# New tokens of the token-major products: 64 high beside 64 low parts in two float32r passes

## The chip, the cores and the metric

One core of a Trainium2 chip runs one program. The time is that of one execution on the device in microseconds (us). Of the core's engines, TensorE (PE) multiplies matrices, VectorE (DVE), ScalarE (ACT) and GpSimd (POOL) work on tiles, and SyncE (SP) issues most DMA transfers. Each engine takes its instructions in its own fixed order and waits at semaphores for the others.

## The reference

One step of a hybrid decoder with two layers, on 512 prompt tokens (one sequence) and 64 new tokens (8 samples of 8), which share all weights; D = 1024, everything in float32. Layer 0 projects its input to the queries, keys and values of sparse attention A (an indexer chooses keys by top-k) and of forgetting attention B, which read paged caches; layer 1 is a gMLP. A ConvFFN follows each. What the change touches is the projection `h @ w` of all 576 tokens, where the result is wanted with tokens in the rows:

```
def project_ab(h, w_in, b_f, pos):
    ...
    qa, ka, va, qi, ki, wi, qb, kb, vb, fb = jnp.split(h @ w_in, offs, axis=-1)
...
def chunk_gate_inputs(h, w_in, lnv_g, lnv_b):
    z = jax.nn.gelu(h @ w_in, approximate=False)
    u, v = jnp.split(z, 2, axis=-1)
    return u, layer_norm(v, lnv_g, lnv_b)
```

Here `h = x*(1+scale)+shift` with a scale and shift for each sequence. The indexer's queries (`qi`), `vb`, `va`, `ka`, `qa` and the gMLP's `v` are the products with tokens in the rows ("token-major"): 1024 columns of w in `w_ab`, 1536 in `w_aa`, 2048 in `w_v`.

## The kernel before

Activations lie feature-major: 1024 features in 8 blocks (kb) of 128 partitions, 576 tokens beside each other, the 512 of the prompt first, then the 64 new ones. A float32 product is made of float32r values: an operand is split into a high part (`xh`, `wh`), rounded by ScalarE, and the low rest (`xl`, `wl`), subtracted by VectorE or GpSimd (`split_to` for activations, `weights` for a unit of 128x1024 weights; L251 casts, L254 subtracts). `mm3` (L283 to L285) then makes three passes: high by high, high by low, low by high. Each of the tiles `wr` (raw weights), `wh` and `wl` has three buffers; a buffer is loaded again when its last reader has finished.

In a token-major product (`token_product`, `token_unit`) the tokens are the stationary operand, 128 at a time, and the weights are streamed; a unit of weights serves 1024/n blocks k of n columns, n = 512 for `w_ab` (two products of 4 units: indexer queries, then values of B), n = 256 for `w_aa` (`project_a`, 6 products of 2 units) and `w_v` (`gmlp`, 8 products of 2 units). Token blocks 0 to 3 go through `mm3`. The last block, tb = 4, has only the 64 new tokens; its product is one plain float32 matmul for each k, of a raw copy `xn` (64 columns) with the raw weights `wr` (L682). Even k add up in PSUM rows 0 to 63, odd k in rows 64 to 127 (`tile_position` chooses the half of the array), and `both_halves` adds the two.

`xn` is written by GpSimd for layer 0 (`modulate`, L430: eight copies of 128x64, one for each kb) and, for the gMLP, by `Norm.finish`, where it is the value before the split. `Norm.finish` runs at each norm that has a successor: into the first FFN, into the gMLP, and into the second FFN. Both norms' splits are L741 (new tokens) and L161/L162 (prompt). The gMLP's first units run at its entrance, mixed with the norm's transposes (L83, L153); from about 1151 us its units follow each other alone.

Behind the `w_ab` product of the indexer's queries hangs a chain: rotary turn (L705 to L708, VectorE), transposes (L721), copies of the new tokens' query rows (L942, GpSimd), their transposes (L945, PE), gathers of indexer keys (L1106, GpSimd's queue), scores (L1109 to L1122), and a top-k on VectorE (from L1048), beside which B's projections and the projections of A run. Pages of the caches are loaded by SyncE meanwhile.

The order on each engine is not written by hand: a scheduler lays it out when the kernel is built, from the program text, priorities and its own simulation of the engines. A change in a few instructions therefore moves others as well.

Of the kernel before, what the change touches and what calls it, by code (L numbers as in the profile page):

```python
# [10 lines left out]
F32 = mybir.dt.float32  # L11
# [48 lines left out]
class Norm:  # L60
# [56 lines left out]
    def finish(self, part):  # L117
# [19 lines left out]
        if part:  # L137
# [8 lines left out]
            nc.vector.tensor_tensor(t, t, wide(self.offs), op=OP.add)  # L146
            net.split_to(*(w[:, :, NP:] for w in self.out), self.xn)
        for k0 in range(0, KB, 2):
            ks = slice(k0, k0 + 2)
# [53 lines left out]
class Net:  # L203
# [217 lines left out]
    def modulate(self, xk, sc1, sh, kb, pool):  # L421
# [7 lines left out]
        nc.vector.tensor_tensor(ts, ts, sh[:, kb, 1:9, None].to_broadcast([P, 8, 8]), op=OP.add)  # L429
        nc.gpsimd.tensor_copy(self.xn[:, kb], t[:, NP:])  # L430
        self.split_to(*(x[:, kb] for x in self.xhl), t)


# [114 lines left out]
    def gmlp(self, x, last, psum, pool, xp, *norm):  # L548

        nc, a, xs, xn = self.nc, self.a, last.xs, last.xn  # L550
        g1 = self.plus_one(1, 2, xp, "g1")
# [19 lines left out]
        def lead():  # L571
            c, u = todo.pop(0)
            if u == 0:
                led[c] = [], [psum.tile([P, 2, 256], F32, name=name, bufs=b) for name, b in (("acc", 4), ("tc", 2))]
            units, accs = led[c]
            units.append(self.weights(a["w_v"][c, u], 1024))
            self.token_unit({tb: accs[tb // 4][:, tb % 2] for tb in (2, 3, 4)}, units[u], u, 256, xs, xn, True, (2, 3, 4))

# [3 lines left out]
        for c in range(8):  # L582
            first = None
            for u in range(2):
# [3 lines left out]
                first = first or psum.tile([P, 2, 256], F32, name="acc", bufs=4)  # L588
                self.token_unit([first[:, 0], first[:, 1]], units[u], u, 256, xs, xn, True, (0, 1))
            accs = [first] + led.pop(c)[1]  # L590
# [73 lines left out]

    def token_unit(self, accs, w, u, n, xs, xn, shared=False, tbs=range(5), between=None):

# [4 lines left out]
        for tb in tbs:  # L671
            for j in range(per):
# [7 lines left out]
                else:  # L680
                    c = 64 * (k % 2)
                    self.nc.tensor.matmul(accs[tb][c:c + NS], xn[:, k], wk[2], start=k < 2, stop=k >= KB - 2,  # L682
                                          tile_position=(0, c))
            if between:
                between()

    def token_product(self, accs, srcs, xs, xn, n, between=None, shared=False, before=None):

        for u, src in enumerate(srcs):
            w = self.weights(src, 1024)  # L690
            if before:
                before(u)
            self.token_unit(accs, w, u, n, xs, xn, shared, between=between)

# [55 lines left out]
    def project(self, keep, pool, room, psum, free):  # L750
# [5 lines left out]
        xs = self.xs = [self.halves(tuple(x[:, kb] for x in self.xhl)) for kb in range(KB)]  # L756
        self.xn = pool.tile([P, KB, NS], F32, name="xn")
        self.sc1 = pool.tile([P, KB, 9], F32, name="sc1")
# [56 lines left out]
        toks = self.five(psum)  # L815
        self.token_product(toks, [a["w_ab"][0, u] for u in range(4)], xs, self.xn, 512, None, False, before)
        qit = self.pair(tmp, [P, 4, NP], "qit")
# [5 lines left out]
        kd = tmp.tile([P, 5, P], F32, name="kd")  # L823
        rt = tmp.tile([P, 5, 64], F32, name="rt8")
        for n, t0, t1 in ((P, 0, 4), (NS, 4, 5)):
# [18 lines left out]
        for ci, name in enumerate(("qi", "vb")):  # L844
            accs = toks
            if ci:
                accs = self.five(psum)
                self.token_product(accs, [a["w_ab"][ci, u] for u in range(4)], xs, self.xn, 512, between)
            for tb in range(5):
# [50 lines left out]
    def project_a(self, pool, psum, xs, between):  # L900
# [3 lines left out]
        for c, name in enumerate(("va", "ka", "qa")):  # L904
            for half in range(2):
                cols = slice(256 * half, 256 * half + 256)
                accs = [psum.tile([P, 2, 256], F32, name="s", bufs=5) for _ in range(3)]
                self.token_product([accs[tb // 2][:, tb % 2] for tb in range(5)], [a["w_aa"][c, half, u] for u in range(2)],
                                   xs, self.xn, 256, between, True)
                for i in range(3):  # L910
# [702 lines left out]
```

## Time and profile before

| | us |
|---|---|
| three timed runs | 1953.62, 1954.88, 1960.26 (median 1954.88) |
| profiled execution, its own time | 1954.99 |
| its span (first to last instruction) | 1952.9 |
| PE busy | 1830.8 (94% of the span), 14456 matmul records |
| DVE, ACT, POOL busy | 1185.3, 736.5, 374.0 |
| mean granted clock of PE | 0.968 of full speed |

The profile shows one execution. A row of the timeline has the start, the duration, the engine, the line, the operation with output and inputs, the shape, and a count where equal instructions follow each other (x8); brackets hold the time that the engine stood idle before the row and what ended it. The end of a matmul is modelled, so the distance from start to start is the better measure. In the trace one float32 matmul stands as two records of L682 each; a float32r matmul as one.

### The profile page before, as it was taken

To read this page: it belongs to the slowest core of one execution; us is meant where nothing else is said; L and a number is where in the kernel's file an instruction comes from. 1 tells how busy PE (TensorE), PEld (TensorE's weight loads), DVE (VectorE), ACT (ScalarE), POOL (GpSimd) and SP (SyncE) were. 2 spreads that over 40 slices of the span, in tenths; PEclk is the share of its full clock that TensorE was granted. 3 is DMA by queue.
4 is the path that set the end of the run, shared out by engine and by line. 5 is a ranking of instruction groups with operands and counts; after the bars stand their busy time and mean duration, and the time that the engine had idled before them with its cause. 6 is when DMAs were issued, how large, how long until landed. Compare 5 with 4: busy or idle time off the path is not lost. (4 is left out here: it accounts for less than half of the span.)

```text
span 1952.9 us, 37037 instructions
## 1 busy us (share of the span) xinstructions
PE 1830.8 (94%) x14456; PEld 1627.1 (83%) x14456; DVE 1185.3 (61%) x2437; ACT 736.5 (38%) x1372; POOL 374.0 (19%) x521
## 2 busy tenths in 40 slices
PE   6889999898889899999999999899998999999996
PEld 4646877555559899999999899799997999999995
DVE  3549963455449754545456953875468555565577
ACT  2323222255444533424344433122224535344543
POOL 2323511110025300100012330430013201010124
PEclk9989999999899999999999999899998999999998
DMA  8446587797864345353543333321222231313242
GB/s 287 128 151 219 179 263 244 238 304 240 279 232 141 118 132 181 126 181 128 193 140 109 107 101 98 94 70 59 82 97 86 71 103 62 102 50 114 87 139 92
DMA packets 140032, 284.39 MB, mean 146 GB/s; under 512 B 32338, under 2 KB 42002, under 8 KB 139794
## 3 DMA queue, kind: packets, MB, share of 16 engines
q1 hardware_dynamic: 139138, 279.67, 43.8%
q0 software_dynamic: 720, 2.36, 0.4%
q8 instruction: 114, 1.87, 0.4%
q14 instruction: 60, 0.49, 0.1%
HBM read 271.04 MB, written 10.94 MB: 144 GB/s over the span
## 5 line engine op out<-in xcount | busy, mean ns | idle before, releaser
L298 PE MATMUL acc<-xh,wh 128*128 128x256 f32 (+1 forms) x1664 | 499.9, 301 | 3.0 <-ACT xh L161 1.7
L298 PE MATMUL acc<-xl,wh 128*128 128x256 f32 (+1 forms) x1664 | 497.5, 299 | 4.8 <-DVE xl L162 4.8
L298 PE MATMUL acc<-xh,wl 128*128 128x256 f32 (+1 forms) x1664 | 496.0, 298 | 6.0 <-DVE wl L254 6.0
L251 ACT CAST wh<-wr 128x1024 fp32r<-128x1024 f32 (+2 forms) x276 | 260.7, 949 | 536.6 <-PE acc L298 371.6
L254 DVE TENSOR_TENSOR wl<-wr,wh 128x1024 fp32r<-128x1024 f32 (+2 forms) x211 | 229.4, 1090 | 240.2 <-ACT wh L251 214.4
L298 PEld LDWEIGHTS acc<-xh,wh 128*128 128x128 f32 x1664 | 319.9, 192 | 11.5 <-issue 6.2
L298 PEld LDWEIGHTS acc<-xh,wl 128*128 128x128 f32 x1664 | 319.9, 192 | 6.6 <-DVE wl L254 6.2
L298 PEld LDWEIGHTS acc<-xl,wh 128*128 128x128 f32 x1664 | 319.9, 192 | 6.2 <-DVE xl L162 6.0
L254 POOL TENSOR_TENSOR wl<-wr,wh 128x1024 fp32r<-128x1024 f32 x65 | 160.5, 2469 | 531.2 <-ACT wh L251 513.4
L298 PE MATMUL acc<-gh,wl 128*128 128x256 f32 (+1 forms) x704 | 207.7, 298 | 1.6 <-DVE wl L254 1.6
L298 PE MATMUL acc<-gl,wh 128*128 128x256 f32 (+1 forms) x704 | 208.8, 298 | 0.0
L298 PE MATMUL acc<-gh,wh 128*128 128x256 f32 (+1 forms) x704 | 207.5, 300 | 0.4 <-ACT gh L740 0.4
L439 DVE SCALAR_TENSOR_TENSOR x<-acc,g,x 128x256 f32<-128x256 f32 x256 | 119.7, 476 | 118.3 <-PE acc L298 112.9
L525 DVE SCALAR_TENSOR_TENSOR y<-up,wc,y 128x592 f32<-128x592 f32 x176 | 150.6, 856 | 34.0 <-ACT y L522 29.9
L298 PEld LDWEIGHTS acc<-gh,wh 128*128 128x128 f32 x704 | 132.4, 189 | 5.5 <-issue 2.9
L298 PEld LDWEIGHTS acc<-gh,wl 128*128 128x128 f32 x704 | 132.6, 189 | 2.9 <-DVE wl L254 1.9
L298 PEld LDWEIGHTS acc<-gl,wh 128*128 128x128 f32 x704 | 133.3, 189 | 0.3 <-DVE gl L741 0.2
L518 POOL COPY tail<-up 128x2 f32<-128x2 f32 x88 | 26.1, 297 | 519.4 <-ACT up L516 519.1
L516 ACT COPY up<-acc 128x256 f32<-128x256 f32 x176 | 65.1, 371 | 130.0 <-PE acc L298 121.8
L283 PE MATMUL s<-wh,xh 128*128 128x256 f32 (+1 forms) x256 | 82.4, 330 | 3.2 <-ACT wh L251 3.2
L522 ACT ACTIVATE y<-up,wc 128x592 f32<-128x592 f32 x88 | 77.8, 884 | 9.2 <-POOL up L514 1.1
L285 PE MATMUL s<-wh,xl 128*128 128x256 f32 (+1 forms) x256 | 81.0, 317 | 0.0
(435 smaller groups left out, 3513.5 us busy)
## 6 DMA issues: line engine op xcount, KB each, us to landing
wr<-in_w_up SPq DMA_DIRECT2D x88, 512.0 KB
wr<-in_w_down SPq DMA_DIRECT2D x32, 512.0 KB
wh<-in_w_mod SPq DMA_DIRECT2D x30, 512.0 KB
wl<-in_w_mod SPq DMA_DIRECT2D x30, 512.0 KB
wr<-in_w_mod SPq DMA_DIRECT2D x28, 512.0 KB
own<-in_kT_b SPq DMA_DIRECT2D x48, 256.0 KB
own<-in_v_b SPq DMA_DIRECT2D x44, 256.0 KB
wr<-in_w_down SPq DMA_DIRECT2D x32, 320.0 KB
```

The costliest lines, as they stand in the source:

```text
L251: nc.scalar.copy(h, r)
L254: (nc.vector if low == "v" else nc.gpsimd).tensor_sub(l, r, h.bitcast(F32))
L283: mm(out, sh, mh, start=start, stop=False)
L285: mm(out, sl, mh, start=False, stop=stop)
L298: mm(acc, w[:, k * P:(k + 1) * P], m, start=i == 0, stop=i == n - 1)
L439: nc.vector.scalar_tensor_tensor(xp, acc[:, :256], g1[:, ob, 0:1], xp, op0=OP.mult, op1=OP.add)
L516: nc.scalar.copy(u[:, 2 + 256 * part:258 + 256 * part], accs[part][:, :256])
L518: nc.gpsimd.tensor_copy(tail[:, blk, 0:2], u[:, NP:NP + 2])
L522: nc.scalar.activation(y[:, :n], u[:, 0:n], AF.Identity, bias=wc[:, 3, blk:blk + 1], scale=wc[:, 0, blk:blk + 1])
L525: nc.vector.scalar_tensor_tensor(y[:, :n], u[:, k:k + n], wc[:, k, blk:blk + 1], y[:, :n], op0=OP.mult, op1=OP.add)
```

## The change

`xn`, where a product reads it, becomes `xst`: for each block k 64 columns of the high parts of the new tokens and beside them 64 columns of the low parts, float32r, copied by GpSimd after the split. The product of the last token block becomes two passes for each k, `xst` (128 columns) by `wh` and by `wl`: rows 0 to 63 of PSUM get the high tokens' products, rows 64 to 127 the low tokens', and `both_halves` adds them as before. `low` by `low` is now included. The raw weights are no longer read by PE. In the norm, `xn` stays as the value before the split and `xst` is new beside it. A scratch tile `rt8` of the projection is replaced by the shared one `rt`.

```diff
@@ -145,6 +145,9 @@
             nc.scalar.copy(x[:, :, NP:], ps)
             nc.vector.tensor_tensor(t, t, wide(self.offs), op=OP.add)
             net.split_to(*(w[:, :, NP:] for w in self.out), self.xn)
+            self.xst = xp.tile([P, KB, 2, NS], F32R, name="xst")
+            for i, w in enumerate(self.out):
+                nc.gpsimd.tensor_copy(self.xst[:, :, i], w[:, :, NP:])
         for k0 in range(0, KB, 2):
             ks = slice(k0, k0 + 2)
             pt = psum.tile([P, 2, 2, P], F32, name="tp", bufs=2)
@@ -427,8 +430,9 @@
         nc.vector.tensor_tensor(ts, xk[:, NP:].rearrange("p (b q) -> p b q", b=8),
                                 sc1[:, kb, 1:9, None].to_broadcast([P, 8, 8]), op=OP.mult)
         nc.vector.tensor_tensor(ts, ts, sh[:, kb, 1:9, None].to_broadcast([P, 8, 8]), op=OP.add)
-        nc.gpsimd.tensor_copy(self.xn[:, kb], t[:, NP:])
         self.split_to(*(x[:, kb] for x in self.xhl), t)
+        for i, x in enumerate(self.xhl):
+            nc.gpsimd.tensor_copy(self.xst[:, kb, i], x[:, kb, NP:])
 
 
     def add_gated(self, x, acc, g1, ob, pool, part):
@@ -547,7 +551,7 @@
 
     def gmlp(self, x, last, psum, pool, xp, *norm):
 
-        nc, a, xs, xn = self.nc, self.a, last.xs, last.xn
+        nc, a, xs, xst = self.nc, self.a, last.xs, last.xst
         g1 = self.plus_one(1, 2, xp, "g1")
 
         ws = pool.tile([P, 8, P], F32, name="ws")
@@ -574,7 +578,7 @@
                 led[c] = [], [psum.tile([P, 2, 256], F32, name=name, bufs=b) for name, b in (("acc", 4), ("tc", 2))]
             units, accs = led[c]
             units.append(self.weights(a["w_v"][c, u], 1024))
-            self.token_unit({tb: accs[tb // 4][:, tb % 2] for tb in (2, 3, 4)}, units[u], u, 256, xs, xn, True, (2, 3, 4))
+            self.token_unit({tb: accs[tb // 4][:, tb % 2] for tb in (2, 3, 4)}, units[u], u, 256, xs, xst, True, (2, 3, 4))
 
 
         for _ in range(3):
@@ -586,7 +590,7 @@
                     lead()
                 units, accs = led[c]
                 first = first or psum.tile([P, 2, 256], F32, name="acc", bufs=4)
-                self.token_unit([first[:, 0], first[:, 1]], units[u], u, 256, xs, xn, True, (0, 1))
+                self.token_unit([first[:, 0], first[:, 1]], units[u], u, 256, xs, xst, True, (0, 1))
             accs = [first] + led.pop(c)[1]
             for i in range(3):
                 n, nb = (P, 2) if i < 2 else (NS, 1)
@@ -662,7 +666,7 @@
 
         return bass.AP(tensor=ap.tensor, offset=ap.offset, ap=[[0, n]] + [list(s) for s in ap.ap[1:]])
 
-    def token_unit(self, accs, w, u, n, xs, xn, shared=False, tbs=range(5), between=None):
+    def token_unit(self, accs, w, u, n, xs, xst, shared=False, tbs=range(5), between=None):
 
 
 
@@ -678,19 +682,19 @@
                     self.mm3(accs[tb], *x, *wk[:2], k == 0 and not (shared and tb % 2),
                              k == KB - 1 and not (shared and tb % 2 == 0))
                 else:
-                    c = 64 * (k % 2)
-                    self.nc.tensor.matmul(accs[tb][c:c + NS], xn[:, k], wk[2], start=k < 2, stop=k >= KB - 2,
-                                          tile_position=(0, c))
+                    x = xst[:, k].rearrange("p i n -> p (i n)")
+                    for i in range(2):
+                        self.nc.tensor.matmul(accs[tb], x, wk[i], start=k + i == 0, stop=k + i == KB)
             if between:
                 between()
 
-    def token_product(self, accs, srcs, xs, xn, n, between=None, shared=False, before=None):
+    def token_product(self, accs, srcs, xs, xst, n, between=None, shared=False, before=None):
 
         for u, src in enumerate(srcs):
             w = self.weights(src, 1024)
             if before:
                 before(u)
-            self.token_unit(accs, w, u, n, xs, xn, shared, between=between)
+            self.token_unit(accs, w, u, n, xs, xst, shared, between=between)
 
     def both_halves(self, acc, out):
 
@@ -754,7 +758,7 @@
         tmp = room.enter_context(tmp)
         self.xhl = self.pair(pool, [P, KB, T], "x")
         xs = self.xs = [self.halves(tuple(x[:, kb] for x in self.xhl)) for kb in range(KB)]
-        self.xn = pool.tile([P, KB, NS], F32, name="xn")
+        self.xst = pool.tile([P, KB, 2, NS], F32R, name="xst")
         self.sc1 = pool.tile([P, KB, 9], F32, name="sc1")
         for q in range(2):
             self.begin(q, pool, tmp, psum)
@@ -813,7 +817,7 @@
                              *xs[k][part], k == 0, k == KB - 1)
 
         toks = self.five(psum)
-        self.token_product(toks, [a["w_ab"][0, u] for u in range(4)], xs, self.xn, 512, None, False, before)
+        self.token_product(toks, [a["w_ab"][0, u] for u in range(4)], xs, self.xst, 512, None, False, before)
         qit = self.pair(tmp, [P, 4, NP], "qit")
 
         smt = pool.tile([P, T], F32, name="tmp", bufs=3)[:80]
@@ -821,7 +825,7 @@
             nc.scalar.copy(smt[:, t0:t1], acc[:80, :t1 - t0])
         raw = tmp.tile([P, 5, 80], F32, name="ev8")
         kd = tmp.tile([P, 5, P], F32, name="kd")
-        rt = tmp.tile([P, 5, 64], F32, name="rt8")
+        rt = pool.tile([P, 512], F32, name="rt", bufs=2)[:, :320].rearrange("p (t d) -> p t d", t=5)
         for n, t0, t1 in ((P, 0, 4), (NS, 4, 5)):
             t = psum.tile([P, 4, 80], F32, name="tp", bufs=2)
             for tb in range(t0, t1):
@@ -845,7 +849,7 @@
             accs = toks
             if ci:
                 accs = self.five(psum)
-                self.token_product(accs, [a["w_ab"][ci, u] for u in range(4)], xs, self.xn, 512, between)
+                self.token_product(accs, [a["w_ab"][ci, u] for u in range(4)], xs, self.xst, 512, between)
             for tb in range(5):
                 n = self.tok(tb)[1]
                 rows = slice(tb * P, tb * P + n)
@@ -906,7 +910,7 @@
                 cols = slice(256 * half, 256 * half + 256)
                 accs = [psum.tile([P, 2, 256], F32, name="s", bufs=5) for _ in range(3)]
                 self.token_product([accs[tb // 2][:, tb % 2] for tb in range(5)], [a["w_aa"][c, half, u] for u in range(2)],
-                                   xs, self.xn, 256, between, True)
+                                   xs, self.xst, 256, between, True)
                 for i in range(3):
                     n, nb = (P, 2) if i < 2 else (NS, 1)
                     res, raw, t = (pool.tile([P, 2, 256], F32, name=k, bufs=b)[:n, :nb]
```

Lines of the changed kernel are 3 to 5 higher than those of the kernel before: L283 to L285 become L286 to L288, L250, L251 and L254 become L253, L254 and L257, L682 becomes L687, L721 becomes L725.

Three places of the order. First PE, at the start of the first `w_ab` product: `s` are the accumulators, `tp` those of a small product beside it. Before:

```order
L283 MATMUL s<-wh,xh 128x512 x4
L682 MATMUL s<-wr,xn 64x512 x4
L283 MATMUL tp<-xh,cums 80x256
L283 MATMUL tp<-xh,cums 80x320
L284 MATMUL s<-wl,xh 128x512
```

and now:

```order
L286 MATMUL s<-wh,xh 128x512 x4
L687 MATMUL s<-wh,xst 128x512
L286 MATMUL tp<-xh,cums 80x256
L286 MATMUL tp<-xh,cums 80x320
L287 MATMUL s<-wl,xh 128x512
...
L687 MATMUL s<-wl,xst 128x512
L687 MATMUL s<-wh,xst 128x512
L687 MATMUL s<-wl,xst 128x512
```

Four products of the new tokens, of two units, stood ahead of the first pass with a low part; now one pass stands there, and the other three of the first unit come some 30 rows later.

Second SP's queue, at the load of the second unit of the second `w_ab` product, with what each issue waits for (PE, Pool, Activation, DVE are the engines, DMAHW the transfers). Before:

```order
L372 DMA wr<-in_w_mod 128x1024 [waits DMAHW6_49,DMAHW5_49,PE_49]
L372 DMA wr<-in_w_mod 128x1024 [waits DMAHW1_49,PE_49]
L833 DMA o_aki_p<-kd 128x4x64 [waits DMAHW7_49,DVE_49]
L833 DMA o_aki_s<-kd 64x64 [waits DMAHW0_49,DVE_49]
L250 DMA wr<-in_w_ab 128x1024 [waits DMAHW2_49,PE_49,Pool_49]
```

and now:

```order
L375 DMA wr<-in_w_mod 128x1024 [waits DMAHW4_49,DMAHW1_49,Pool_49]
L253 DMA wr<-in_w_ab 128x1024 [waits DMAHW5_49,DMAHW2_49,Pool_49]
L375 DMA wh<-in_w_mod 128x1024 [waits PE_49]
L375 DMA wl<-in_w_mod 128x1024 [waits DMAHW7_49,PE_49]
L375 DMA wr<-in_w_mod 128x1024 [waits DMAHW5_49,DMAHW0_49,Pool_49]
L837 DMA o_aki_p<-kd 128x4x64 [waits DVE_49]
```

The load of `w_ab` went ahead of the output `o_aki_p`, and a `wr` buffer waits for GpSimd's subtraction only, no longer for PE.

Third GpSimd, at the norm before the gMLP: `wl` are low parts of weights, the rows L168 the residual of the next sublayer. Before:

```order
L254 TENSOR_TENSOR wl<-wr,wh 128x1024 [waits DVE_49,DMAHW0_49,PE_49,Activation_49]
L254 TENSOR_TENSOR wl<-wr,wh 128x1024 [waits DMAHW1_49,PE_49,Activation_49]
L254 TENSOR_TENSOR wl<-wr,wh 128x1024 [waits DVE_49,DMAHW2_49,PE_49,Activation_49]
L168 TENSOR_SCALAR x<-x,ga,ba 128x576 [waits DVE_49] x5
```

and now:

```order
L257 TENSOR_TENSOR wl<-wr,wh 128x1024 [waits DVE_49,DMAHW0_49,PE_49,Activation_49]
L150 COPY xst<-xh 128x8x64 [waits Activation_49]
L150 COPY xst<-xl 128x8x64 [waits DVE_49]
L257 TENSOR_TENSOR wl<-wr,wh 128x1024 [waits DMAHW1_49,PE_49,Activation_49]
L257 TENSOR_TENSOR wl<-wr,wh 128x1024 [waits DMAHW2_49,PE_49,Activation_49]
L171 TENSOR_SCALAR x<-x,ga,ba 128x576 [waits DVE_49] x5
```

The two copies stand ahead of the last two subtractions, and wait for the norm's split on ScalarE and VectorE.

## Rows read from the trace of the kernel before

**Rows 1.** The page, busy time: engine, us, share of the span, instructions.

```profile
PE 1830.8 (94%) x14456; PEld 1627.1 (83%) x14456; DVE 1185.3 (61%) x2437; ACT 736.5 (38%) x1372; POOL 374.0 (19%) x521
```

**Rows 2.** Line L682: ns of one (min, median, max), first and last start, shapes.

```profile
L682 PE MATMUL s<-wr,xn x128: 379/379/1116, 36.7 to 365.4; 128*64 128x256 f32 x96, 128*64 128x512 f32 x32
...
L682 PE MATMUL tc<-wr,xn x128: 379/379/689, 1118.9 to 1228.7; 128*64 128x256 f32 x128
```

**Rows 3.** Windows: length; PE, PEld, DVE, ACT, POOL busy; clock, DMA share, GB/s.

```profile
230.00:366.00 136.00, 128.30 (x1345) 100.92 (x1348) 76.06 (x181) 30.40 (x63) 26.88 (x24) 0.96 0.73 244
366.00:590.00 224.00, 190.54 (x1810) 120.59 (x1800) 118.44 (x400) 107.61 (x298) 33.23 (x26) 0.94 0.84 259
...
1151.00:1229.00 78.00, 78.00 (x630) 70.05 (x628) 26.33 (x43) 21.49 (x32) 0.00 (x0) 1.00 0.30 96
```

**Rows 4.** Timeline of PE in the steady v projection: start, us, operation.

```profile
1151.16 0.28 PE L284 MATMUL acc<-wl,xh 128*128 128x256 f32 x1
1151.28 0.28 PE L285 MATMUL acc<-wh,xl 128*128 128x256 f32 x1
1151.49 1.08 PE L682 MATMUL tc<-wr,xn 128*64 128x256 f32 x8
...
1152.73 0.28 PE L284 MATMUL acc<-wl,xh 128*128 128x256 f32 x1
```

**Rows 5.** Timeline of PE at the start of the first projection.

```profile
34.72 2.08 PE L283 MATMUL s<-wh,xh 128*128 128x512 f32 x4 [3.22 <-ACT wh L251]
36.73 3.68 PE L682 MATMUL s<-wr,xn 128*64 128x512 f32 x8
```

**Rows 6.** Timeline of PE later in the first projection.

```profile
68.18 0.40 PE L284 MATMUL s<-wl,xh 128*128 128x512 f32 x1
68.42 0.39 PE L285 MATMUL s<-wh,xl 128*128 128x512 f32 x1
68.74 1.08 PE L682 MATMUL s<-wr,xn 128*64 128x512 f32 x4
...
78.94 1.08 PE L682 MATMUL s<-wr,xn 128*64 128x512 f32 x4 [2.53 <-DVE tmp L698]
...
83.72 1.08 PE L682 MATMUL s<-wr,xn 128*64 128x512 f32 x4 [2.48 <-DMA wr<-in_w_ab]
```

**Rows 7.** Timeline of POOL in the first projection and at the key gathers.

```profile
34.74 2.37 POOL L254 TENSOR_TENSOR wl<-wr,wh 128x1024 fp32r<-128x1024 f32 x1 [6.66 <-ACT wh L251]
...
90.55 1.16 POOL L942 COPY row<-ro 64x512 f32<-64x512 f32 x2 [2.05 <-DVE ro L708]
...
96.54 0.99 POOL L1106 DMA_INDIRECT row<-in_kidx,kx  x1 [1.21 <-PE tp L945]
```

**Rows 8.** Timeline of SP's queue, 79 to 82 us.

```profile
80.09 0.35 SPq L250 DMA_DIRECT2D wr<-in_w_ab  x1
```

**Rows 9.** Timeline of PE at the entrance to the gMLP.

```profile
1118.69 0.33 PE L83 MATMUL tc<-c_ident,x 128*128 128x128 f32 x1 [2.10 <-DVE x L439]
...
1121.97 0.42 PE L283 MATMUL acc<-wh,xh 128*128 128x256 f32 x1
...
1122.78 0.28 PE L284 MATMUL acc<-wl,xh 128*128 128x256 f32 x1
...
1131.33 1.94 PE L682 MATMUL tc<-wr,xn 128*64 128x256 f32 x14
1133.20 1.09 PE L153 MATMUL tp<-c_ident,rt 128*128 128x128 f32 x8
```

**Rows 10.** Line L430: ns of one (min, median, max).

```profile
L430 POOL COPY xn<-tmp x8: 236/236/749, 14.6 to 58.8; 128x64 f32<-128x64 f32 x8
```

**Rows 11.** Timeline of DVE at the norm before the gMLP.

```profile
1111.72 5.21 DVE L162 TENSOR_TENSOR xl<-tmp,xh 128x512 fp32r<-128x512 f32 x2
...
1119.79 0.68 DVE L162 TENSOR_TENSOR xl<-tmp,xh 128x512 fp32r<-128x512 f32 x1
```

**Rows 12.** Timeline of POOL in the same place.

```profile
1111.17 5.21 POOL L254 TENSOR_TENSOR wl<-wr,wh 128x1024 fp32r<-128x1024 f32 x2 [3.27 <-ACT wh L251]
```

## The prediction

> **What bounds the kernel now.** I read the page's busy table first: TensorE (PE) works 1830.8 us of a span of 1952.9, 94% [rows 1]. The reader is to see that no other engine comes near, so work taken off PE is worth its length wherever PE has a queue, and nothing where PE waits. Next I looked for the line that changes, L682, by its instructions: 256 matmul records in two places, the attention projections (the accumulators `s`) and the gMLP's v projection (`tc`) [rows 2]. A product of 64 tokens with raw float32 weights appears as two records, so this is 128 products: 16 of 512 columns (eight units of two), 48 and 64 of 256 columns (groups of four). Then I took the windows of three stages to see whether PE is the limit there: 78.00 of 78 us in the steady v projection, 128.30 of 136 in the projections of A beside the top-k on VectorE, 190.54 of 224 in the attention over pages, where the DMA engines are busy 0.84 of the time [rows 3]. So a saving counts in full in the first, mostly in the second, and in the third only if what feeds it also comes earlier. Last I read the order of instructions around each kind of group.
>
> **The product itself, 256 columns.** In the steady v projection the last float32r pass before a group starts at 1151.28 and the second one after it at 1152.73 [rows 4]. These 1.45 us hold two float32r passes, which follow each other every 0.12 us there (1151.16 to 1151.28), so a group of four products costs 1.45 - 0.24 = 1.21 us. The change makes it eight float32r passes, 8 x 0.12 = 0.96. Saving: 0.25 us a group. Much of this is the change of mode: in the long run of 14 records at 1131.33 seven products take 1133.20 - 1131.33 = 1.87 us, 0.27 each, against 0.24 for two passes [rows 9]. A new pass has 128 columns in its stationary operand where the raw product had 64; I take the neighbours' 0.12, since they load 128 too and also move 256 columns.
>
> **512 columns.** Passes follow each other every 0.24 us (68.18, 68.42). The group of two products starts 68.74 - 68.42 - 0.24 = 0.08 late and takes 1.08; four passes take 0.96 [rows 6]. Saving: 0.2 us a group of two.
>
> **Sum by stage.**
>
> *First projection stage.* The first group of four products runs after a wait, at the lower clock: four float32r passes take 2.08 us (0.52 each, twice the 0.24) and the raw products 3.68 [rows 5]. Now one new pass stands there, three stand some 20 matmuls later. The low part of the first unit is ready at 34.74 + 2.37 = 37.11 [rows 7], so PE goes straight on to it. I take -1.0 (not the 3.68 - 0.96 = 2.7 of full clock, because the clock has to rise again first). The groups at 60.37 and 68.74: -0.4. The raw weights are no longer read by PE: `wr` becomes free when its low part has been subtracted, and SyncE issues the load of the next unit, now at 80.09 [rows 8], before the two small outputs ahead of it. The two PE waits of 2.53 and 2.48 us around the groups at 78.94 and 83.72 [rows 6] change: the second goes with the earlier load, but twelve or more of its unit's matmuls are now ahead of the key and query transposes, and VectorE's rotary chain waits for those transposes. What the stage hands on is the index chain: POOL copies the query rows at 90.55 and issues the second key gather at 96.54, which waits for the transposes (L945) behind 20 matmuls of 512 columns, 20 x 0.24 = 4.8 us [rows 7]. These matmuls now run ahead, so the gather comes up to 1.8 us sooner after the copies. Everything after it to the top-k is a chain of latencies. I take -1.5 for the stage's end; bounds -4 (all of it handed on) and +2 (the transposes 2 us later by the matmuls placed ahead). The second w_ab product, groups at 135.49 and 148.30: -0.4.
>
> *Projections of A, 228 to 366.* Twelve groups, 12 x 0.25 = 3.0. PE is busy 94% there [rows 3], 2.8; I take -2.5, because the next stage is fed by page loads. Bounds 0 (the pages set the end) and -3.0.
>
> *Entrance to the gMLP, 1118 to 1134.* Four groups, 32 passes: at full clock -1.0. PE comes out of a wait of 2.10 us at the lower clock: a pass at 1121.97 takes 0.42 instead of 0.28 [rows 9]. Both kinds of work pay that. I take -0.9; bounds -2 and +1.5, since the order of these 16 products and of the transposes L153 (now after some 60 passes instead of 46 passes and nine products) is another one.
>
> *Steady v projection.* Twelve groups of eight records, one in each unit, 12 x 0.25 = -3.0, PE full [rows 3]: nothing hides it. Bounds -2.8 and -3.2.
>
> *New copies.* In `modulate` eight copies of 128x64 become sixteen, at a median of 0.236 us [rows 10]. POOL waits for most of them anyway, and the product of a unit needs them only at its end: 0, and at worst 8 x 0.24 = 1.9 if each delays a weight split behind it. In each of the three norm finishes two copies of 128x8x64 are new and nothing is taken away; only the gMLP's tile is read by a product. The trace has no such copy. By width the nearest is 64x512 at 0.58 each (two in 1.16) [rows 7]; by pieces, eight of 128x64, 1.9. I take 0.6, as the instruction is one. Six make 3.6 us of POOL, between 2.4 us subtractions. VectorE is held while POOL subtracts: two subtractions `xl` that take 0.68 alone take 5.21 beside two of POOL [rows 11, 12]. So part of the copies becomes VectorE time on the way to PE. I take +0.8 of the 3.6; bounds 0 and, at 1.9 a copy, all held, 11.4.
>
> By the Trainium skill, "SBUF — State Buffer", section "Who interferes with whom", a VectorE instruction with two SBUF inputs and a GpSimd instruction that reads SBUF exclude each other for a whole instruction. The trace agrees: 5.21 for two, beside POOL's 5.21 for two. By that rule alone all 3.6 would be VectorE's, and the time 2.8 higher, 1950.2.
>
> Sum, with the first stage by its end alone: -1.5 - 0.4 - 2.5 - 0.9 - 3.0 + 0.8 = -7.5. The profiled execution took 1954.99 us (2.1 beside its span), the median run 1954.88, which is the same. Prediction: 1954.9 - 7.5 = 1947.4.
>
> **Rivals.**
>
> *The attention part hides its gain.* For: DMA 0.84 busy from 366 to 590, and the top-k on VectorE fills the stretch before. Against: PE has few gaps from 230 to 366. Then only -0.9 - 3.0 + 0.8 = -3.1 is left: 1951.8.
>
> *The first stage gives more.* The waits of 2.53 and 2.48 us both go without a new one; 5.0 instead of 1.5: 1943.9. Against: VectorE's rotary steps are the next wait.
>
> *The new copies hold VectorE at the norm finishes: slower.* Each of six copies takes 1.9 and stands before an `xl` that PE waits for; PE then also falls to the lower clock. One such wait now costs 4 us of lower clock at the gMLP entrance (1118.69 to 1122.8) [rows 9], some 2 us lost. Price 11.4 + 3 x 2 = 17.4 against -8.3: +9.1, 1964. It decides from about 0.7 us a copy with the clock, or 1.4 without. Against: the longest PE wait there is for x, not for these copies, and PE has other work queued.
>
> *The passes are no cheaper.* Break-even for 256 columns is 1.21 / 8 = 0.151 us a pass. At that the sum is 0 to +1: 1955.5. Against: 0.12 in hundreds of neighbours of the same shape.
>
> **Chances.** Forecast 0.53, attention hides 0.17, first stage gives more 0.16, copies 0.10, no cheaper 0.04. What a measurement tells from no change is about 0.3%, 5.9 us: below 1949.0 is faster, above 1960.7 slower. Of the forecast's share seven tenths lie below 1949.0, as its uncertain terms (-1.5, -2.5, -0.9) spread by some 3 us together; with the bigger first stage and little of the others: faster 0.55, same 0.36, slower 0.09 (most of the copies' case and a little for the new order elsewhere). Range: down to 1940 (bigger first stage with its bound of -4 and the gMLP's -2), up to 1957, which holds the hidden attention and the passes that are no cheaper and leaves out the copies.
>
> **What would show it.** Right: groups of eight passes every 0.12 in the v projection, and a unit there 0.25 us shorter; the end of the v projection some 4 us earlier against its start; the first top-k step about 1.5 us earlier. Copies of `xst` on POOL of about 0.6 us. Wrong: a pass above 0.15 us, `xl` subtractions longer at the norm finishes with PE waiting on them, or a start of the FFN after attention that has not moved while the projections of A end earlier.

## The result and the profile after

The changed kernel takes 1944.53 us (median of six, 1939.46 to 1949.6) against 1954.56 (six, 1950.94 to 1960.26); ratio 0.9947, 95% interval 0.9927 to 0.9966. A second series (e10) gave 1941.61, ratio 0.9922 (0.9898 to 0.9947). So it is 7 to 20 us shorter, by the two intervals, most likely 10 to 15; forecast were 7.5. Both kernels scatter by 10 us from run to run, and the traced execution was the changed kernel's slowest, 1949.6 (span 1947.8). Single traces are therefore read by stage below.

The page's busy table of the changed kernel, to be held against [rows 1]:

```profile
PE 1826.5 (94%) x14456; PEld 1647.5 (85%) x14456; DVE 1182.4 (61%) x2437; ACT 737.1 (38%) x1372; POOL 387.7 (20%) x535
```

PE is 4.3 us shorter and GpSimd 13.7 longer. As many matmul records as before: two passes take the place of one float32 product, which was two records.

PE in the steady v projection of the changed kernel, as in [rows 4]: start, us, operation.

```profile
1153.07 0.28 PE L288 MATMUL acc<-wh,xl 128*128 128x256 f32 x1
1153.19 0.28 PE L687 MATMUL tc<-wh,xst 128*128 128x256 f32 x1
1153.31 0.28 PE L687 MATMUL tc<-wl,xst 128*128 128x256 f32 x1
...
1154.03 0.28 PE L687 MATMUL tc<-wl,xst 128*128 128x256 f32 x1
1154.15 0.28 PE L286 MATMUL acc<-wh,xh 128*128 128x256 f32 x1
```

Eight passes from 1153.19 to 1154.15 take 0.96 us, 0.12 each, with no delay on either side. From group to group it is 6.72 us, eleven times, where it was 6.95.

The start of the first projection, PE of the changed kernel, as in [rows 5]:

```profile
32.71 1.20 PE L286 MATMUL s<-wh,xh 128*128 128x512 f32 x4 [1.34 <-ACT wh L254]
33.74 0.40 PE L687 MATMUL s<-wh,xst 128*128 128x512 f32 x1
38.43 0.77 PE L286 MATMUL tp<-xh,cums 128*80 128x256 f32 x2 [4.29 <-ACT xh L744]
```

After one new pass PE stands idle for 4.29 us, until ScalarE has made the high part of the next block. In the kernel before, the raw products ran in that place until 40.4, here at the lower clock [rows 5]. In its second trace (e9), where the first passes start at 32.61, they took 1.94 us at full clock, and the small product behind them started at 36.19:

```profile
36.19 0.50 PE L283 MATMUL tp<-xh,cums 128*80 128x256 f32 x2 [0.51 <-ACT xh L740]
```

So the high part itself came about 2 us later in the changed kernel. GpSimd and VectorE show why; before:

```profile
37.59 0.24 POOL L430 COPY xn<-tmp 128x64 f32<-128x64 f32 x1 [0.48 <-DVE tmp L429]
37.78 2.34 POOL L254 TENSOR_TENSOR wl<-wr,wh 128x1024 fp32r<-128x1024 f32 x1
...
37.32 0.21 DVE L429 TENSOR_TENSOR tmp<-tmp,mod 128x64 f32<-128x64 f32 x1
```

and in the changed kernel:

```profile
32.74 4.85 POOL L257 TENSOR_TENSOR wl<-wr,wh 128x1024 fp32r<-128x1024 f32 x2 [3.23 <-ACT wh L254]
...
35.32 2.35 DVE L432 TENSOR_TENSOR tmp<-tmp,mod 128x64 f32<-128x64 f32 x1
```

The copy `xn` stood between the two subtractions and waited for VectorE's last addition of the next block. The copies `xst` wait for the split behind that addition, so the two subtractions follow each other, and the addition takes 2.35 us instead of 0.21: it ends with the second of them, and only then can ScalarE round the high part. After the wait PE runs at the lower of its two levels, 1.2 GHz, a pass every 0.43 us (columns of the window as in [rows 3]):

```profile
38.99 0.63 PE L287 MATMUL s<-wl,xh 128*128 128x512 f32 x1
39.42 0.63 PE L288 MATMUL s<-wh,xl 128*128 128x512 f32 x1
...
38.50:43.50 5.00, 5.00 (x13) 4.03 (x14) 2.28 (x5) 0.67 (x1) 2.25 (x4) 0.50 0.98 381
```

All seven traces with the new passes in this product have the wait (4.28 to 4.65) and then six to eleven passes 0.43 apart; the five traces with the old order on GpSimd (both of the kernel before, e1, e4 and e5) wait at most 0.52 at that place.

The copies of `xst` on GpSimd in the changed kernel: ns of one (min, median, max), first and last start. L435 is in `modulate`, L150 in the norms; [rows 10] had the copy that they replace.

```profile
L435 POOL CAST xst<-xh x8: 762/823/826, 15.5 to 59.5; 128x64 fp32r<-128x64 f32 x8
L435 POOL CAST xst<-xl x8: 233/236/492, 17.0 to 60.4; 128x64 fp32r<-128x64 f32 x8
```

```profile
L150 POOL CAST xst<-xh x3: 611/890/1074, 623.6 to 1482.9; 128x512 fp32r<-128x512 f32 x3
L150 POOL CAST xst<-xl x3: 669/737/739, 627.9 to 1484.6; 128x512 fp32r<-128x512 f32 x3
```

The copy of a high part takes 0.82 where the same copy of a low part takes 0.24: it starts when VectorE subtracts `xl`, and is held for that.

The largest change stands where the forecast had only a third of it, in the projections of A. SyncE's issues before (start, duration of the issue, transfer), the last two loads of weights `w_aa` and the loads of page data into `wr` that follow:

```profile
318.30 0.39 SPq L250 DMA_DIRECT2D wr<-in_w_aa  x1
...
335.55 0.36 SPq L250 DMA_DIRECT2D wr<-in_w_aa  x1
...
356.14 0.85 SPq L269 DMA_DIRECT2D wr<-in_v_b  x2
...
359.30 0.91 SPq L269 DMA_DIRECT2D wr<-in_kT_b  x2
...
372.74 0.37 SPq L269 DMA_DIRECT2D wr<-in_kT_b  x1
```

The same loads of the changed kernel:

```profile
304.26 0.52 SPq L253 DMA_DIRECT2D wr<-in_w_aa  x1
...
350.13 0.86 SPq L272 DMA_DIRECT2D wr<-in_v_b  x2
...
353.29 0.85 SPq L272 DMA_DIRECT2D wr<-in_kT_b  x2
...
358.16 0.92 SPq L272 DMA_DIRECT2D wr<-in_kT_b  x2
```

The last weights are asked for at 304.26 instead of 335.55, the first pages into `wr` 6 us and the third pair 14.6 us earlier. What stood behind the late weights is seen on ScalarE and PE of the kernel before:

```profile
324.25 1.04 ACT L251 CAST wh<-wr 128x1024 fp32r<-128x1024 f32 x1 [4.33 <-DMA wr<-in_w_aa]
```

```profile
325.26 0.44 PE L721 MATMUL tp<-c_ident,ro 64*128 64x64 f32 x2 [3.15 <-DVE ro L708]
```

and on PE of the changed kernel:

```profile
323.06 0.34 PE L725 MATMUL tp<-c_ident,ro 64*128 64x64 f32 x2
```

A cast waited for weights there, and PE stood 3.15 us before a transpose; now it waits for nothing at that transpose. That the matmuls of the late unit are what fills the time now is argued from the order.

**By stage.** Each instruction of VectorE, ScalarE and GpSimd is paired with its partner in the first trace of the kernel before (same line, operation and output, same count). The table has the median shift in us of the instructions that start there between 200 and 230 (top-k), 352 and 362 (end of the projections of A), 700 and 720 (after attention and the entrance to the FFN), 1090 and 1104 and 1240 and 1260 (around the v projection), all counted from the first instruction as in the rows; the last column is the difference of the spans.

```
                                  200    352    700   1090   1240    end
before, second trace (e9)        -2.9   -1.2   -1.8   -1.9   -2.0   -1.7
gMLP only (e1)                   -3.0   -1.6   -0.9   -0.9   -2.5   -4.9
scratch tile only (e4)           -1.3   -0.5   +6.9   +6.8   +6.9   +6.7
changed, first trace             +1.1   -6.0   -4.9   -4.5   -7.7   -5.1
changed, second trace (e10)      -0.1   -7.7  -10.0   -9.9  -13.1  -10.2
attention only (e2)              +0.2   -7.5  -11.9  -12.1  -12.2  -12.3
copies in one norm (e3)           0.0   -6.6  -10.6  -10.8  -13.9  -13.5
copies in one norm (e11)         -0.7   -7.7  -12.1  -12.2  -14.8  -14.5
the same, on ScalarE (e8)        -0.4   -7.9  -10.5  -10.7  -14.2  -13.7
release of wr only (e5)          -1.9   -6.1   -7.8   -7.9   -5.4   -6.3
passes, wr held (e12)            +1.6   +4.6   +4.9   +4.8   +3.8   +5.5
first product raw (e6)           -2.3  -11.0   -3.4   -3.5   -6.7   -6.3
both w_ab products raw (e7)      -4.9  -12.7  -11.3  -11.4  -14.6  -13.5
```

Kernels whose attention is that of before (the first trace, e9 and e1) stand at 0 to -3.0 at 200 and 0 to -1.6 at 352; means -2.0 and -0.9. The changed kernel (twice) and e2, e3, e11 have means +0.1 at 200, -7.1 at 352, -9.9 at 700. Some times in the expectations (370 and 383 for the pages, 215 to 357, 362 to 700) count from the start of the trace, 10.2 to 10.8 us ahead of the first instruction.

### The profile page after: what moved, and what is told of

Read it like the earlier page. It is cut to its first block, busy times and chain, and to the rows that moved or that the text cites. A ratio compares the mean times of both kernels' runs of the same rounds, so it can differ in the third digit from the quotient of the medians.

```text
span 1947.8 us, 37052 instructions
## 1 busy us (share of the span) xinstructions
PE 1826.5 (94%) x14456; PEld 1647.5 (85%) x14456; DVE 1182.4 (61%) x2437; ACT 737.1 (38%) x1372; POOL 387.7 (20%) x535
## 4 chain that ended last, share of the span: by engine, by line
PE 70%; DVE 15%; DMA 3%; issue 2%; SPq 1%; ACT 1%; POOL 1%; DVEq 0%; ACTq 0%; POOLq 0%
PE acc L301 51%; PE s L1313 2%; PE acc L288 2%; PE acc L287 1%; PE acc L286 1%; PE tc L378 1%; PE o L1347 1%; DVE tmp L162 1%; DVE wl L257 1%; PE s L286 1%; DVE x L443 1%; PE s L287 1%; PE s L288 1%; PE o L1266 1%; DVE z L615 1%
## 5 line engine op out<-in xcount | busy, mean ns | idle before, releaser
L254 ACT CAST wh<-wr 128x1024 fp32r<-128x1024 f32 (+2 forms) x276 | 260.7, 949 | 516.1 <-PE acc L301 366.6
L257 DVE TENSOR_TENSOR wl<-wr,wh 128x1024 fp32r<-128x1024 f32 (+2 forms) x211 | 230.7, 1095 | 241.8 <-ACT wh L254 215.5
L257 POOL TENSOR_TENSOR wl<-wr,wh 128x1024 fp32r<-128x1024 f32 x65 | 160.5, 2470 | 517.5 <-ACT wh L254 488.6
L286 PE MATMUL s<-wh,xh 128*128 128x256 f32 (+1 forms) x256 | 80.9, 323 | 1.3 <-ACT wh L254 1.3
L287 PE MATMUL s<-wl,xh 128*128 128x256 f32 (+1 forms) x256 | 81.9, 320 | 0.1
L288 PE MATMUL s<-wh,xl 128*128 128x256 f32 (+1 forms) x256 | 81.2, 317 | 0.0
```

The costliest lines, as they stand in the source:

```text
L254: nc.scalar.copy(h, r)
L257: (nc.vector if low == "v" else nc.gpsimd).tensor_sub(l, r, h.bitcast(F32))
L286: mm(out, sh, mh, start=start, stop=False)
L287: mm(out, sh, ml, start=False, stop=False)
L288: mm(out, sl, mh, start=False, stop=stop)
```

## Experiments

**e1, only the gMLP changed; e2, only the attention changed.** `token_unit` keeps both forms and takes the one that the tile's shape asks for (the central part of the edit):

```diff
+                elif len(xst.shape) == 3:
+                    c = 64 * (k % 2)
+                    self.nc.tensor.matmul(accs[tb][c:c + NS], xst[:, k], wk[2], start=k < 2, stop=k >= KB - 2,
+                                          tile_position=(0, c))
                 else:
                     x = xst[:, k].rearrange("p i n -> p (i n)")
```

> Two float32r passes only in the gMLP's v projection, with the copies of all three norms; the attention projections keep the raw product and the tile rt8. Theory A (the passes save what they are shorter by wherever PE is full, and most of the 10 us that the whole change gained comes from the attention part): steady v projection 2.9 us shorter, entrance to the gMLP within 0.5, the copies at the norms cost about 1, so 1952.5 against 1954.6, between 1951 and 1954. Theory B (the attention part gained nothing of its own, its runs differ by chance): this kernel has all of the gain, 1945 to 1948.

> Two float32r passes only in the attention projections (w_ab and w_aa), raw product in the gMLP, no copies in the norms. Theory A: 6 to 9 us faster than before, about 1947, with the projections of A ending 5 us earlier in the trace (at about 361 instead of 366). Theory B: within 2 us of before.

e1: 1954.22, ratio 0.9987 (0.9971 to 1.0003). e2: 1943.99, ratio 0.9933 (0.9906 to 0.9959). Theory B is out: the attention part has its own gain and nearly all of it, more than the 6 to 9 us that theory A gave it. e1 lies just above the 1951 to 1954 of its theory A, and by its interval it may be no change at all; its trace gains 1.6 in the v projection.

**e3 and e11, the copies in the one norm that the gMLP reads.**

```diff
-            self.xst = xp.tile([P, KB, 2, NS], F32R, name="xst")
-            for i, w in enumerate(self.out):
-                nc.gpsimd.tensor_copy(self.xst[:, :, i], w[:, :, NP:])
+            if self.nxt == (1, 0):
+                self.xst = xp.tile([P, KB, 2, NS], F32R, name="xst")
+                for i, w in enumerate(self.out):
+                    nc.gpsimd.tensor_copy(self.xst[:, :, i], w[:, :, NP:])
```

> The changed kernel, but the copies of 64 high and 64 low parts are made only in the norm whose tile the gMLP reads; the two other norms make none (four copies on GpSimd less, PE's order unchanged). Theory A with copies that hold VectorE: 1 to 2 us faster than the changed kernel, 1943; the step of +1.2 us that the changed kernel shows at the entrance to the second FFN is gone. Rival: that step is TensorE's clock and not the copies, then no difference from the changed kernel (within 1 us) and the step stays.

> The kernel with the copies in one norm only, on the same chip as e10. Theory that dead copies hold VectorE on the way to PE: 1 to 2 us faster than e10. Rival that they lie in GpSimd's and VectorE's idle time: within 1 us of e10.

e3: 1941.99, ratio 0.9919 (0.9893 to 0.9945). e11 beside e10, on one chip: 1940.08, 0.9927 (0.9905 to 0.9949), against 1941.61, 0.9922 (0.9898 to 0.9947). No difference can be told: the medians are 1.5 us apart, the means of the six runs 0.1, and the intervals are 10 us wide, so neither the theory's 1 to 2 us nor the rival is out. Their traces differ at one place, the second FFN's entrance (1440 to 1590): the changed kernel loses 1.1 and 1.3 us there, e3, e11 and e8 gain 1.5. So the step is gone, as the theory said. But e1 has the same copies as the changed kernel and gains 1.5 there too. The windows (columns as in [rows 3]) of the changed kernel, and of e1 at the same work, show the clock:

```profile
1486.40:1494.40 8.00, 8.00 (x41) 8.00 (x42) 6.62 (x26) 3.32 (x5) 0.00 (x0) 0.71 0.00 0
```

```profile
1492.10:1500.10 8.00, 8.00 (x57) 8.00 (x56) 6.34 (x25) 3.32 (x5) 0.00 (x0) 1.00 0.00 0
```

PE is busy all 8 us in both, with 41 matmuls at a granted clock of 0.71 and with 57 at 1.00: after the same wait of 2.7 us the one runs longer at the lower level, 1.2 GHz. The second trace of the changed kernel has 0.69 there, e3 and e11 1.00. So the step goes with the clock, and the copies alone do not make it; why the changed kernel, in both its traces, has the lower clock there remains open.

**e4, only the shared scratch tile.**

```diff
-        rt = tmp.tile([P, 5, 64], F32, name="rt8")
+        rt = pool.tile([P, 512], F32, name="rt", bufs=2)[:, :320].rearrange("p (t d) -> p t d", t=5)
```

> The kernel before with only the scratch tile rt8 replaced by the shared rt. Theory A: within 2 us of before, 1953 to 1956. Rival (the gain in attention comes from the shared scratch tile and the order that follows from it): 4 us or more faster.

1960.5, ratio 1.0013 (0.9997 to 1.0029). It gives nothing, and its median lies 5 us above that of the kernel before, outside the 1953 to 1956 of theory A; its trace is even with before at 352 and 7 us later after the attention over pages.

**e5, the release of `wr` without the passes.**

```diff
-                    self.nc.tensor.matmul(accs[tb][c:c + NS], xn[:, k], wk[2], start=k < 2, stop=k >= KB - 2,
+                    self.nc.tensor.matmul(accs[tb][c:c + NS], xn[:, k], wk[0].bitcast(F32), start=k < 2, stop=k >= KB - 2,
                                           tile_position=(0, c))
```

> The kernel before, its plain float32 product of the new tokens kept as it is in shape and count, but with the rounded high part wh for its weights instead of the raw weights wr (it leaves out the weights' low parts for the new tokens). PE's work is that of before; what changes is that a wr buffer is free as soon as its low part has been subtracted. Theory C (a good part of the attention's gain is the earlier release of wr, by which weight and page loads start earlier): projections of A end 2 to 4 us earlier than before (before: about 366), the fourth set of page loads into wr goes out near 370 instead of 383, and the time is 2 to 6 us below before, about 1951. Theory A' (the passes alone): within 2 us of before, 1955.

1952.38, ratio 0.9994 (0.9981 to 1.0007). The stage does more than theory C says: the last product of the projections of A starts at 359.3 instead of 365.4, and from 200 to 352 the trace gains 4.2 us where the kernels with the old attention lose 1.0. SyncE's issues and PE's transpose in e5:

```profile
302.86 0.51 SPq L250 DMA_DIRECT2D wr<-in_w_aa  x1
...
350.04 0.86 SPq L269 DMA_DIRECT2D wr<-in_v_b  x2
...
358.48 0.92 SPq L269 DMA_DIRECT2D wr<-in_kT_b  x2
```

```profile
321.70 0.31 PE L721 MATMUL tp<-c_ident,ro 64*128 64x64 f32 x2 [0.37 <-DVE ro L708]
```

They are those of the changed kernel, with before's products; the pages expected near 370 from the trace's start are the row at 358.48. The total hardly moves: 2.1 us by the medians, inside theory C's 2 to 6 at its edge, but by the interval it may be no change. The v projection loses 2.5 us again (its new order has one group more, still 6.95 apart), and the traced run was near its fastest.

**e12, the passes without the release.** A small float32 matmul reads `wr` in each of the 12 units of the projections of A (the central part of the edit; `hold` is given only there, else as e3):

```diff
                         self.nc.tensor.matmul(accs[tb], x, wk[i], start=k + i == 0, stop=k + i == KB)
+                        if i == 0 and hold is not None and j == per - 1:
+                            self.nc.tensor.matmul(hold[:NS, :8], xst[:, k, 0].bitcast(F32), wk[2][:, :8], start=False, stop=False)
```

> Copies in one norm only, two passes everywhere, but in the projections of A one small plain float32 matmul of 8 columns in each of the 12 units reads the raw weights between the last block's two passes (it adds that product once more to 8 columns of the new tokens' result), so that wr is held as in the kernel before. It costs PE about 0.1 to 0.2 us a unit. Theory C (the release of wr gives about 5 us by the end of the projections of A, the passes 3): from 215 to 357 us this kernel gains only 1 to 2 us on the trace of before instead of 6 to 7, the wait of 3 us for ro at the transposes is back, the fourth set of pages into wr goes out 14 us after the third as before. Rival (the passes' order makes the gain, not the release): 4 us or more gained there.

1955.51, ratio 1.0003 (0.9988 to 1.0018): the whole gain is gone, 15.4 us against e11 on the same chip. PE and SyncE in e12:

```profile
330.10 0.45 PE L728 MATMUL tp<-c_ident,ro 64*128 64x64 f32 x2 [2.06 <-DVE ro L715]
```

```profile
340.75 0.36 SPq L254 DMA_DIRECT2D wr<-in_w_aa  x1
...
362.58 0.86 SPq L273 DMA_DIRECT2D wr<-in_v_b  x2
...
366.49 0.85 SPq L273 DMA_DIRECT2D wr<-in_kT_b  x2
...
380.24 1.89 SPq L273 DMA_DIRECT2D wr<-in_kT_b  x2
```

The wait is back, the third pair of pages goes out 13.8 us after the second as before (13.4), not 4.9 as in the changed kernel. From 200 to 352 e12 loses 3.0 us, where a gain of 1 to 2 was expected. Part of this is the price of holding, expected at 0.1 to 0.2:

```profile
241.17 0.28 PE L688 MATMUL s<-wh,xst 128*128 128x256 f32 x1
241.38 0.28 PE L690 MATMUL s<-wr,xst 128*64 128x8 f32 x2
241.59 0.39 PE L688 MATMUL s<-wl,xst 128*128 128x256 f32 x1
241.82 0.28 PE L287 MATMUL s<-wh,xh 128*128 128x256 f32 x1
```

The pass ahead of the small product starts at 241.17, the pass behind it at 241.59 and the next instruction at 241.82, 0.65 us where two passes take 0.24. That is 0.41 a unit, 4.9 in all. If all of it is on the path, e12 would gain 1.9 without it, 2.9 against the old attention, so the passes' 3.0 would show with `wr` held too; how much of the price is on the path no run tells. The rival, 4 us or more from the passes and their order, is out in either case. In the total the two experiments do not agree on the release: taking it away costs some 10 us beyond the price, giving it alone (e5) brings 2.

**e6 and e7, the first or both `w_ab` products as before** (`raw=True` for that product, else as e3):

```diff
+                elif raw:
+                    c = 64 * (k % 2)
+                    self.nc.tensor.matmul(accs[tb][c:c + NS], xst[:, k, 0].bitcast(F32), wk[2], start=k < 2, stop=k >= KB - 2,
+                                          tile_position=(0, c))
```

> The kernel with copies in one norm only, but the first product (w_ab, indexer queries, 16 records of 512 columns) is made as before: plain float32 with raw weights, of the high parts of the tokens (it leaves out their low parts there). Theory D (the raw products covered PE's wait for the next block's high part at 34 to 38 us, which the changed kernel shows as 4.3 us idle, so the change gains nothing in the first stage): PE works without that gap, the query transposes come 1 to 2 us earlier than in the changed kernel, and the total is the same as with copies in one norm (1942) within 2 us. Rival: the first stage is worth what was forecast (1.5 us): 1943.5 or more.

> As e6, and the second w_ab product also plain float32 with raw weights; only the projections of A and the gMLP's v projection use the two passes. Theory A/C: projections of A still give their 3 us of passes and the wr release, so the time is about 1943 (1941 to 1946). Rival (the release at w_ab makes the gain): 1948 or more.

e6: 1949.07, ratio 0.9969 (0.9954 to 0.9984). e7: 1941.19, 0.9939 (0.9925 to 0.9952). Theory D is half right: PE still waits 2.65 us for the same high part, but at 200 e6 stands 2.3 us and e7 4.9 us ahead, where the seven traces with new passes in both `w_ab` products stand at +0.2 in the mean (-0.7 to +1.6). (Those with the old products in both, e4 and e5 included: 0 to -3.0, mean -1.8.) So the passes in `w_ab` do not help the first stages; in these single traces they cost 2 to 5 us up to the top-k, and e7's total, as expected, shows that they give nothing later either. e6's total missed its expectation and by its number meets the rival's 1943.5 or more; but e6 is 11.0 ahead at 352 and gives 7.6 back in the attention over pages, and e7, where both products are raw, has the gain. Why e6 gives it back is open.

**e8, the copies on ScalarE** (`nc.scalar.copy` for `nc.gpsimd.tensor_copy`, else as e3).

> Copies in one norm only, and all copies of the 64 high and 64 low columns made by ScalarE instead of GpSimd. Theory: GpSimd's copies of high parts take 0.82 in the first stage where VectorE subtracts at the same time, and ScalarE is busy 38%; copies there hold nobody: the same as with copies in one norm on GpSimd or up to 1 us faster, 1941 to 1942. Rival: ScalarE's casts of weights stand behind the copies and PE waits for them: 1 us or more slower.

1941.34, ratio 0.9937 (0.9921 to 0.9954): no difference from e3 can be told, as expected. Its trace has GpSimd's two subtractions behind each other (4.85) and the 4.28 us wait of PE as well: it is where the copies no longer stand that delays the high part, not the engine that makes them.

**e9 and e10, both kernels once more.**

> The kernel before once more, for a second trace of it: how far two executions of one kernel differ by stage. Theory: up to the end of the projections of A within 1.5 us of the first trace, in the attention over pages (362 to 700 us) up to 5 us either way, after it within 1.5 us. If two traces of one kernel differ by more than 4 us before 362, the stage table says nothing of the release of wr.

> The changed kernel once more, beside e11: its trace again about 5.5 us ahead of the first trace of before at 352 to 362 us (4 to 8), its attention over pages up to 5 us different from its first trace. Time 1944 (1941 to 1948).

e9: 1953.04, ratio 0.999 (0.9977 to 1.0004). The two traces of before differ by 2.9 us at 200, more than the 1.5 expected, and by 1.2 to 2.0 from 352 on; those of the changed kernel by 1.7 at 352 and 5.1 at 700. e10 kept what was expected of it at 352 (4 to 8) and in its time. A step of 6 to 8 us at 352 in five traces is thus more than the scatter; what the attention over pages adds is not certain in any one of them.

## Why the prediction was right in its time and not in its terms

The forecast 1947.4 lay in its range, 3 us above the median of the first series and 6 above that of the second: 7.5 us were forecast, 10.4 and 15.2 measured by the two ratios. By its own steps, with means of the traces against the kernels with the old attention:

- *The product.* 0.25 us a group of four was forecast, 6.95 - 6.72 = 0.23 measured. Right. The v projection with its entrance was to give 3.9 (-0.9 and -3.0): from 1090 to 1240 it gave 2.6 to 3.5 in e3, e6, e7, e8, e10, e11 and the first trace, but 1.6 in e1 and 1.0 in e12. Twelve groups of 0.23 are 2.8, so the entrance gave at most 0.7, and in e1 and e12 it lost.
- *First stage, -1.5 and -0.4.* Wrong in sign: about +2 at the top-k (+0.1 against -2.0). Instead of 1.5 us earlier, the first top-k step came at 127.3 to 128.9 in the seven traces with the new passes, and at 125.6 to 127.9 in the four with `w_ab` as before. The step that failed is "The low part of the first unit is ready at 34.74 + 2.37 = 37.11 [rows 7], so PE goes straight on to it." The transposed small product (`tp<-xh,cums`) stands ahead of it and waits for the next block's high part; the raw products had filled most of that wait, and the order that went on record shows that row. The wait also grew by some 2 us, since the copies of `modulate`, which the sum put at 0, no longer stand between GpSimd's two subtractions; and PE came out of it at the lower clock. The query transposes then start at 85.65 instead of 80.15, behind all matmuls of the last unit, which the prediction had as its bound of +2. With the same early load and the old products (e5) they start at 82.26 and the top-k at 125.0, so the early load is not what costs. What the wait, the clock and the passes' place cost each is not separated: e6 and e7 have the late high part too and are not behind.
- *Projections of A, -2.5.* Right in the passes, and a term was missing: from 200 to 352 the changed kernels gain 7.2 where the old attention loses 1.0, so 8.2. e5 alone gains 4.2 there, 5.2 against the old. The rest is 3.0, the 3.0 of the 12 groups. The prediction saw the release of `wr` and priced it only at the first stage, where the wait for `w_ab` stands. The same buffers carry `w_aa` and then the pages.
- *Attention over pages, 0.* From 352 to 700 the shift of the changed kernel, e2, e3, e10 and e11 is +1.1 to -4.4, mean -2.8; with the old attention it is 0, -0.6 and +0.7. Pages that start earlier would explain a gain, but e6, whose pages start earlier still, loses 7.6, and so does e4 (7.4), whose pages start as before. This remains open.
- *Copies, +0.8.* Those at the norms took 0.61 to 1.07 each against the 0.6 taken; their cost at the end is not measurable (e3, e11, e8). By the Trainium skill, "SBUF — State Buffer", section "Who interferes with whom", 2.8 more were to come; the exclusion is seen in the copies themselves (0.82 beside VectorE's subtraction, 0.24 alone), and no run shows it in the end for the copies at the norms. Where it did reach PE is the first stage, in the addition of 2.35 us.
- *Rivals.* "Attention hides its gain" is refuted by e1 and e2. The slower one did not come, though the copies were long enough for it: at 3 x 2 us of clock its sum breaks even at (8.3 - 6) / 6 = 0.4 us a copy, not at the 0.7 that it names, and the copies took more than either in the mean (0.79). No trace shows PE waiting for them at the norms. "The first stage gives more" went the other way. The largest effect, the release in the projections of A, was no rival. And the range's lower end of 1940 is not what its two bounds give: 1947.4 - 2.5 - 1.1 = 1943.8.

So the time was luck in part: a gain of 5.7 us missed in the projections of A, and the 2.8 behind them that remain open, stood against a first stage wrong by nearly 4 and a gMLP too large by 1.

## What to carry to other kernels

An operand that a matmul reads is also a buffer that the matmul holds: when the only late reader of a tile goes, look along the whole queue that refills it, not only at the next wait, and test it apart from the arithmetic (read another tile of the same shape; or hold the buffer with a small read). Before a slow instruction is removed, see what it runs beside: work that fills another wait is free, and taking it away gains nothing. The same holds for a short one on an engine with time to spare: here a copy of 0.24 us between two long subtractions had let another engine through, and without it an addition of 0.21 took 2.35. Where runs scatter by 10 us, shifts by stage of paired instructions, with a second trace of the same kernel for the scatter, tell more than totals.

## What the runs showed that was not expected

- A plain float32 matmul of 64 tokens by 8 columns between float32r passes costs 0.41 us (0.65 for it and the two passes around it instead of 0.24), a third of what a group of four products of 256 columns cost (1.21). How much of it is the change to and fro, and how much the product itself, is not separated.
- Two kernels with the same copies differ by some 2.5 us at the second FFN's entrance, behind an equal wait, with the granted clock (0.71 and 1.00 over 8 us of a busy PE); the two traces of the changed kernel agree (0.71 and 0.69).
